# Keeping the two parts of split weights in DRAM across blocks, with the q-k-v staging and the weight sums moved

## The chip, the cores and the metric

The kernel runs on one core of a Trainium2 chip. The metric is the device time of one launch in microseconds (us), the median of three runs, lower being better.

## The reference

One step of a one-layer hybrid decoder, on a prompt of 2048 tokens and 32 sample tokens (8 sequences of 4), width 1024, in float32:

```python
h = rmsnorm(x, n1)
z = h @ w_in                      # splits into hq, hf, hi, hg, sq, sk, sv, ga, gb
f = lb + (1 - lb) * sigmoid(hf)
o_hg, s_new = hgrn_recurrence(hq, log(f), 1 - f, hi, s0, chunk=64)   # 4 heads of 128
y_a = (rmsnorm(o_hg, hg_norm_w) * silu(hg)) @ w_up_a
q, k, v = rotary(sq), rotary(sk), sv                 # 8 query heads, 2 key heads, of 64
y_b = sliding_window_attention_with_sinks(q, k, v, window=128) @ w_up_b
m = sigmoid(ga) * y_a + sigmoid(gb) * y_b
x = x + m @ w_o
x = x + square(relu(rmsnorm(x, n2) @ w_ff1)) @ w_ff2
y = rmsnorm(x, normf_w)
```

It also returns the last keys and values of the window and the recurrent states.

## The kernel before, in words

The prompt is cut into four blocks of 512 tokens, two to a superblock; block 3 carries the 32 sample tokens too. Every product is done in three matmuls of a rounded float32 format: a matrix is split into a high part (a cast) and a low part (what the cast leaves over), and high x high, low x high and high x low are added up. The activations are split as they are made; the weights are split each time that they are loaded.

A superblock runs as follows.

- The norm of its tokens, and their transposes. In superblock 0 the tiles of block 1 (`xo0` to `xo3`) follow block 0's: each is loaded, normed (a Square with sum on ScalarE, a scaling on ScalarE), transposed on TensorE, scaled into a buffer `ho` of which there is one, stored to DRAM as `hraw`, and added up with block 0's tile into the five operand sums of a Strassen product (`first_sums`: `zS1`, `zS2`, `zS3`, `zS4`, `zA22`). In superblock 1 these sums are made from `hraw`, loaded by POOL as `za11`, `za12`, `za21`, `za22`.
- The attention's k-v columns (`skv`, two weight units) and q columns (`sq`, four) of the even block, staged in a tile `zqk` and stored to DRAM.
- "z": the Strassen product of both blocks with the columns of `w_in` for the recurrence's queries and the two gates. Its weights are called `w1r` raw, `w1B` and `w1T` split; a phase that needs only the first activations and `w1B` comes first, then the one with the sums.
- The mixer of the even block: rotary and attention, `hi`, `hf`, `hg` (four units each), the recurrence, `ub` and `ua` (up-projections, four units each, with the gates: on VectorE the product with the gate at L1065, on POOL the addition of both at L1090), `wo` (eight units).
- The mixer of the odd block, which first makes `sq` and `skv` itself.
- The feed-forward part of both blocks, again by Strassen. The sums of its second weight matrix are made once, in block 0: sixteen sums, each of four loads (L508), four subtractions on VectorE (L510 to L513) and four stores to DRAM (L515), loads and stores issued by POOL.

A weight unit is 512 KB, a tile of 128x1024. It is loaded raw by SyncE (`r_...`, L144), cast by ScalarE to the high part (`h_...`, L230) and subtracted by VectorE to the low part (`l_...`, L231). All three tiles come from a pool of twelve. In the chip's program each engine works through its queue in order. A scheduler sets that order when the kernel is built, from the order of the code, the dependences and the free slots of the pools.

Of the kernel before, what the change touches and what calls it, by code (L numbers as in the profile page):

```python
# [38 lines left out]
def F(ap):  # L39
    return ap.bitcast(F32)  # L40
# [3 lines left out]
def tile_hybrid_step(  # L44
# [92 lines left out]
    v_last = cp.tile([P, P], F32, name="v_last")  # L137
    k_last = cp.tile([P, P], F32, name="k_last")

    def unit(parts, a, name):  # L140
        raw = wtile(F32, "r_" + name)
        raw3 = raw.rearrange("p (a b) -> p a b", a=a)
        for (p0, p1, src) in parts:
            nc.sync.dma_start(raw3[p0:p1], src)  # L144
        wh, wl = split_w(raw, name)
        return wh.rearrange("p (a b) -> p a b", a=a), wl.rearrange("p (a b) -> p a b", a=a)

    def split_w(raw, name):
        wh, wl = wtile(F32R, "h_" + name), wtile(F32R, "l_" + name)
        split_out(wh, wl, raw)  # L150
        return wh, wl
# [2 lines left out]
        nc.scalar.copy(hi, F(lo))  # L154
        nc.vector.tensor_tensor(lo, F(lo), F(hi), ALU.subtract)  # L155

    def unit_rows(w, k0, a, c0, nc_, name):
        src = w[k0 * P:(k0 + a) * P, c0:c0 + nc_].rearrange("(k p) c -> p k c", p=P)
        return unit([(0, P, src)], a, name)

    def gemm_T(ps, n, wts, acts, t0):
        nk = len(wts)
# [20 lines left out]
    def gemm_NK(w, c0, outs, acts, name, hook=None):  # L183
        for i in range(KD // 2):
            uh, ul = unit_rows(w, 2 * i, 2, c0, 512, f"{name}{i}")
            for (ps, r0, nr) in outs:
                for kk in range(2):
                    k = 2 * i + kk
                    lh = acts[k][0][:, r0:r0 + nr]
                    ll = acts[k][1][:, r0:r0 + nr]  # L190
                    nc.tensor.matmul(ps[0:nr], lh, uh[:, kk, :], start=(k == 0), stop=False)  # L191
                    nc.tensor.matmul(ps[0:nr], lh, ul[:, kk, :], start=False, stop=False)  # L192
# [332 lines left out]
    for bi in range(nblk):  # L525
# [70 lines left out]
        def colN512(c0, name, fn, hook=None):  # L596
            rings = [mm_ps, mm_ps, hg_ps, hg_ps, sw_ps]
            ps = [rings[i](f"ps_{name}_{t[3]}") for i, t in enumerate(tiles)]
            gemm_NK(w_in, c0, [(p, t[1], t[2]) for p, t in zip(ps, tiles)], h_acts, name, hook)
            for p, (kind, r0, nr, c) in zip(ps, tiles):  # L600
                fn(p[0:nr], kind, c, nr)

# [82 lines left out]
            return x.rearrange("p (g v d) -> p v g d", g=G, v=NKV)  # L685

        if not odd:
            stage = (op(3, F32, f"zqk_{B}") if sb else op(2, F32, f"zqk_{B}"))[:, 0:768 * ncb].rearrange("p (c e) -> p c e", e=768)

            def step():  # L690
                for _ in range(3):
# [1 line left out]
                        todo.pop(0)()  # L693

            def st_skv(ps, kind, c, nr):
                nc.scalar.copy(stage[:, c, 512:768], ps)

            def st_sq(ps, kind, c, nr):
                nc.scalar.activation(qk_out(stage[:, c, 0:512]), qk_in(ps), AF.Copy, scale=HD ** -0.5)
                nc.scalar.dma_start(zqk[sb][c * P:(c + 1) * P, :], stage[:, c, :])  # L700

            colN(C_SQ + 512, f"skv{B}", st_skv)
            colN512(C_SQ, f"sq{B}", st_sq, lambda i: step())
# [10 lines left out]
            with tc.tile_pool(name=f"zp{sb}", bufs=1, reuse_waits="tile") as zp:  # L714
                def z_fin(u, blk, x, ps=None):
                    o, nh = int(blk[1]) - 1, int(blk[2]) - 1
                    zi = 2 * u.n + nh
                    if zi >= HH:
                        nc.scalar.activation(x, x if ps is None else ps, AF.Tanh, scale=0.5)
                    elif ps is not None:  # L720
                        nc.scalar.copy(x, ps)
                    q = nc.scalar if zi >= HH else nc.gpsimd
                    rs = slice(zi * P, (zi + 1) * P)
                    c0, c1 = u.t0, u.t0 + u.ln
                    if o == 0:
# [342 lines left out]
        for j in range(KD):  # L1068
            if j % 2 == 0:
                ub = unit(  # L1070
                    [(kv * HD, (kv + 1) * HD, w_ub[kv * 256:(kv + 1) * 256, j * P:j * P + 256].rearrange("(k p) c -> p k c", p=HD)) for kv in range(NKV)],
                    4, f"ub{B}{j}")
# [9 lines left out]
        a_acts = [(oa[:, 0, k, :], oa[:, 1, k, :]) for k in range(4)]  # L1082
        mT = [op(2 + g, F32R, f"m{g}_{B}")[:, 0:8 * T].rearrange("p (s k t) -> p s k t", s=2, k=4) for g in range(2)]
        for j in range(KD):
            if j % 4 == 3:
                sum_next()
            if j % 2 == 0:
                ua = unit_rows(w_ua, 0, 4, j * P, 256, f"ua{B}{j}")
# [95 lines left out]
        if odd:  # L1184
            rings = (sw_ps, sw_ps, hg_ps, hg_ps, mm_ps)
            ps = [rings[i](f"wo{B}0_{t[3]}") for i, t in enumerate(tiles)]
            gemm_NK(w_o, 0, [(p, t[1], t[2]) for p, t in zip(ps, tiles)], m_acts, f"wo{B}0")
            for p, t in zip(ps, tiles):
                wo_out(t, p, 0)
            us_ = [unit_rows(w_o, 2 * i, 2, 512, 512, f"wo{B}1{i}") for i in range(KD // 2)]  # L1190
# [9 lines left out]
        else:  # L1200
# [21 lines left out]
            for cg in range(2):  # L1222
                rings = ((sw_ps, sw_ps, hg_ps, hg_ps), (mm_ps, mm_ps, sw_ps, sw_ps))[cg]
                ps = [rings[i](f"wo{B}{cg}_{t[3]}") for i, t in enumerate(tiles)]
                gemm_NK(w_o, cg * 512, [(p, t[1], t[2]) for p, t in zip(ps, tiles)], m_acts, f"wo{B}{cg}", hook)
                for p, t in zip(ps, tiles):
                    wo_out(t, p, cg)
            while todo:
# [293 lines left out]
```

## Time and profile before

| | us |
|---|---|
| Median of 3 runs | 2984.28 (2983.39 to 2984.38) |
| The profiled execution | 2989.63 |
| Its span, first to last instruction | 2987.9 |
| TensorE busy | 2825.5 (95%) |
| VectorE busy | 1775.6 (59%) |
| ScalarE busy | 1182.0 (40%) |
| POOL busy | 550.3 (18%) |

The mean granted clock of TensorE is 0.977 of its full speed. The DMA engines moved 492.78 MB. A time with no unit beside it is a position in the span, in us from its start: block 0's norms and q-k-v run to about 80, z of superblock 0 to 315, block 0's mixer to 560, block 1's to 830, the feed-forward part to 1495; z of superblock 1 to 1720, block 2's mixer to 2005, block 3's to 2285.

In the profile PE is TensorE, DVE VectorE, ACT ScalarE and SP SyncE; a q behind the name is the engine's sequencer, where DMAs are issued. In a timeline row stand the start, the duration, the engine, the line, the operation, output and inputs, and in brackets how long the engine had been idle and what released it. Names there are shortened: `h_ubb` is any of the block's `ub` units.

### The profile page before, as it was taken

The page shows a single profiled execution, that of the slowest core. Times are in us where ns is not written, and L with a number is a line of the kernel's source. Part 1 is how long each engine was busy: PE and PEld are TensorE (multiplying, and loading weights), DVE is VectorE, ACT ScalarE, POOL GpSimd, SP SyncE. Part 2 cuts the span into 40 slices and gives each one's busy share as a digit, 9 for nine tenths or more (in the row PEclk, how much of TensorE's full clock was granted, in tenths as well). Part 3 has the DMA queues.
Part 4 walks back from the last instruction along what each step waited for, and adds up shares of the span by engine and source line. Part 5 has one row for each costly group of instructions (what it writes and reads, how often), then busy time and mean ns, then how long its engine had stood idle before and what let it go on. Part 6 is the DMA issues. An engine that isn't in the chain of part 4 may idle for free. (4 is left out here: it accounts for less than half of the span.)

```text
span 2987.9 us, 50439 instructions
## 1 busy us (share of the span) xinstructions
PE 2825.5 (95%) x20087; PEld 2446.0 (82%) x20087; DVE 1775.6 (59%) x2877; ACT 1182.0 (40%) x2257; POOL 550.3 (18%) x957
## 2 busy tenths in 40 slices
PE   6799888999989999999999998999998999999998
PEld 5578666868878887888889967877887999999998
DVE  3664476457578775555575355525766877654446
ACT  3434332344343334554354443334424333344433
POOL 1130324121222221010220020120113333310001
PEclk8899899999999999999999999999998999999999
DMA  4473556424465447667563323442356444485552
GB/s 155 136 244 118 176 191 233 161 82 141 157 214 173 155 153 259 214 208 252 175 205 105 118 86 119 135 151 87 99 165 188 151 158 138 148 283 190 179 193 102
DMA packets 320180, 492.78 MB, mean 165 GB/s; under 512 B 28332, under 2 KB 193224, under 8 KB 319928
## 3 DMA queue, kind: packets, MB, share of 16 engines
q1 hardware_dynamic: 252048, 305.18, 32.5%
q0 software_dynamic: 48064, 155.58, 14.8%
q10 hardware_dynamic: 19832, 28.79, 2.7%
q8 instruction: 158, 2.59, 0.4%
q14 instruction: 78, 0.64, 0.1%
HBM read 351.96 MB, written 138.51 MB: 164 GB/s over the span
## 5 line engine op out<-in xcount | busy, mean ns | idle before, releaser
L1358 PE MATMUL f<-f2S,hw2T 128*128 128x264 f32 (+1 forms) x576 | 184.1, 320 | 0.0
L1360 PE MATMUL f<-f2S,lw2T 128*128 128x264 f32 (+1 forms) x576 | 183.5, 319 | 0.0
L1359 PE MATMUL f<-f2S,hw2T 128*128 128x264 f32 (+1 forms) x576 | 183.5, 319 | 0.0
L155 DVE TENSOR_TENSOR lw2T<-lw2T,hw2T 128x1024 fp32r<-128x1024 f32 x64 | 78.3, 1225 | 118.9 <-ACT hw2T L154 118.4
L238 PE MATMUL fB_f<-S,w1T_f 128*128 128x264 f32 (+1 forms) x384 | 123.1, 321 | 5.3 <-ACT c_f L300 4.4
L1358 PE MATMUL f<-f2A,h_w2B 128*128 128x264 f32 (+1 forms) x384 | 122.7, 320 | 0.5 <-ACT c_f L1251 0.5
L1359 PE MATMUL f<-f2A,h_w2B 128*128 128x264 f32 (+1 forms) x384 | 122.4, 319 | 0.1
L239 PE MATMUL fB_f<-S,w1T_f 128*128 128x264 f32 (+1 forms) x384 | 122.3, 319 | 0.0
L1360 PE MATMUL f<-f2A,l_w2B 128*128 128x264 f32 (+1 forms) x384 | 122.3, 319 | 0.0
L240 PE MATMUL fB_f<-S,w1T_f 128*128 128x264 f32 (+1 forms) x384 | 122.2, 319 | 0.0
L154 ACT CAST hw2T<-lw2T 128x1024 fp32r<-128x1024 f32 x64 | 67.2, 1050 | 132.8 <-DMA lw2T<-w_T 129.8
L1358 PEld LDWEIGHTS f<-f2S,hw2T 128*128 128x128 f32 x576 | 108.4, 188 | 7.6 <-DVE hw_ab L416 0.3
L1359 PEld LDWEIGHTS f<-f2S,hw2T 128*128 128x128 f32 x576 | 108.4, 188 | 7.3
L1360 PEld LDWEIGHTS f<-f2S,lw2T 128*128 128x128 f32 x576 | 108.0, 188 | 7.6
L155 DVE TENSOR_TENSOR f2S<-f2S 128x1024 fp32r<-128x1024 f32 (+1 forms) x64 | 79.3, 1241 | 54.7 <-ACT f2S L154 54.2
L231 DVE TENSOR_TENSOR l_w2B<-rw2B,h_w2B 128x1024 fp32r<-128x1024 f32 x48 | 58.8, 1225 | 81.6 <-ACT h_w2B L230 70.7
L230 ACT CAST w1T_f<-w1r_f 128x512 fp32r<-128x512 f32 x128 | 77.1, 619 | 70.5 <-PE fB_f L240 27.6
L231 DVE TENSOR_TENSOR w1T_f<-w1r_f,w1T_f 128x512 fp32r<-128x512 f32 x128 | 87.4, 688 | 23.9 <-ACT w1T_f L230 23.7
L1263 POOL DMA_DIRECT2D u_S<-s_f x144 | 77.7, 540 | 120.1 <-DVE s_f L1258 96.9
L1263 POOL DMA_DIRECT2D u_A<-c_f x104 | 56.2, 541 | 226.4 <-DVE c_f L1247 225.4
L154 ACT CAST f2S<-f2S 128x1024 fp32r<-128x1024 f32 (+1 forms) x64 | 68.0, 1064 | 53.0 <-DMA f2S<-u_S 52.9
L230 ACT CAST h_w2B<-rw2B 128x1024 fp32r<-128x1024 f32 x48 | 50.5, 1052 | 96.2 <-DMA rw2B<-w_ff 92.9
(833 smaller groups left out, 9684.3 us busy)
## 6 DMA issues: line engine op xcount, KB each, us to landing
w1r_f<-w_ff SPq DMA_DIRECT2D x64, 512.0 KB
lw2T<-w_T SPq DMA_DIRECT2D x64, 512.0 KB
rw2B<-w_ff SPq DMA_DIRECT2D x48, 512.0 KB
w1r_z<-w_in SPq DMA_DIRECT2D x40, 512.0 KB
f2S<-u_S SPq DMA_DIRECT2D x32, 528.0 KB
ws<-w_ff POOLq DMA_DIRECT2D x64, 256.0 KB, 4.8
r_wob<-w_o SPq DMA_DIRECT2D x32, 512.0 KB
f2S<-u_S SPq DMA_DIRECT2D x32, 512.0 KB
```

Of the source, the lines that this page charges most:

```text
L154: nc.scalar.copy(hi, F(lo))
L155: nc.vector.tensor_tensor(lo, F(lo), F(hi), ALU.subtract)
L230: nc.scalar.copy(dh, src)
L231: nc.vector.tensor_tensor(dl, src, F(dh), ALU.subtract)
L238: nc.tensor.matmul(ps, wh, ah, start=(first and k == 0), stop=False, skip_group_check=not first)
L239: nc.tensor.matmul(ps, wh, al, start=False, stop=False, skip_group_check=not first)
L240: nc.tensor.matmul(ps, wl, ah, start=False, stop=(last and k == 3), skip_group_check=not first)
L1263: nc.gpsimd.dma_start(us[o][u.n // 4][u.n % 4 * P:(u.n % 4 + 1) * P, u.t0:u.t0 + u.ln], y_)
L1358: nc.tensor.matmul(ps, wh, ah, start=first, stop=False, skip_group_check=cont)
L1359: nc.tensor.matmul(ps, wh, al, start=False, stop=False, skip_group_check=cont)
L1360: nc.tensor.matmul(ps, wl, ah, start=False, stop=lastk, skip_group_check=cont)
```

## The change

Three things are changed.

1. The units of `hi`, `hf`, `hg`, `ub`, `ua` and `wo` are split in block 0, those of `sq` and `skv` in block 1. Both parts are then stored to DRAM (`ws_...`, the high part on ScalarE's queue, the low part on POOL's), 34 units in all. The blocks after that load both parts, 2 x 512 KB, into the tiles `h_...` and `l_...`, with no raw tile, no cast and no subtraction. That holds for 96 units. The units of z and of the feed-forward part are loaded and split as before.
2. The staging of q, k and v of the even block was one tile in the slot of an activation operand (that of `zA22` in block 0, of `zS3` in block 2). It is now four tiles of the weight pool, one for each 128 tokens.
3. Ten of the sixteen sums are begun in z of superblock 0, where it was five, and block 0's mixer starts fewer by hand. The scheduler places the other six between z and block 0's gates.

```diff
+    wsd = {}
+
-    def unit(parts, a, name):
-        raw = wtile(F32, "r_" + name)
...
-        wh, wl = split_w(raw, name)
+    def unit(parts, a, name, key=None):
+        if key in wsd:
+            wh, wl = wtile(F32R, "h_" + name), wtile(F32R, "l_" + name)
+            nc.sync.dma_start(F(wh), wsd[key][0])
+            nc.sync.dma_start(F(wl), wsd[key][1])
+        else:
+            raw = wtile(F32, "r_" + name)
...
+            wh, wl = split_w(raw, name)
+            if key is not None:
+                wsd[key] = [tc.dram_tile([P, 1024], F32, name=f"ws_{key}_{i}") for i in range(2)]
+                nc.scalar.dma_start(wsd[key][0], F(wh))
+                nc.gpsimd.dma_start(wsd[key][1], F(wl))
...
-            wh, wl = unit_rows(w_in, 0, KD, c0 + h * P, P, name)
+            wh, wl = unit_rows(w_in, 0, KD, c0 + h * P, P, name, f"c{c0 + h * P}")
...
-            us = [unit_rows(w_in, 4 * i, 4, c0, 256, f"{name}{i}") for i in range(2)]
+            us = [unit_rows(w_in, 4 * i, 4, c0, 256, f"{name}{i}", f"c{c0}_{i}" if bi else None) for i in range(2)]
...
-            stage = (op(3, F32, f"zqk_{B}") if sb else op(2, F32, f"zqk_{B}"))[:, 0:768 * ncb].rearrange("p (c e) -> p c e", e=768)
+            stage = {}
...
             def st_skv(ps, kind, c, nr):
-                nc.scalar.copy(stage[:, c, 512:768], ps)
+                stage[c] = wtile(F32, f"zqk_{B}{c}")
+                nc.scalar.copy(stage[c][:, 512:768], ps)
...
                 def z_hook():
-                    if sb == 0 and len(sums) > NP - 5:
+                    if sb == 0 and len(sums) > NP - 11:
...
-            if j % 4 == 3:
+            if odd and j % 4 == 3:
                 sum_next()
...
-                    todo += [lambda g=g, k=k: reload(g, k), sum_next]
+                    todo.append(lambda g=g, k=k: reload(g, k))
```

The callers of `unit` for `ub`, `ua` and `wo` pass a key in the same way.

Three places show how the instructions stand now. First ScalarE's queue at the start of block 0, before: the last splits of the first sums (`zS2_0` to `zS4_0` from `xo0`), then the cast of the second `skv` unit, the evictions of `skv` into the staging tile, and the first `sq` unit.

```order
L230 CAST zS2_0_408<-fs0_412 128x4x128
L230 CAST zS3_0_409<-hw_ab010_385 128x4x128
L230 CAST zS4_0_411<-hw_ab000_110 128x4x128
L230 CAST h_skvb01_242<-r_skvb01_240 128x1024
L696 COPY zqk_b0_233<-ps_skvb0_0_246 128x256
L696 COPY zqk_b0_233<-ps_skvb0_1_272 128x256
L696 COPY zqk_b0_233<-ps_skvb0_2_298 128x256
L696 COPY zqk_b0_233<-ps_skvb0_3_324 128x256
L230 CAST h_sqb00_356<-r_sqb00_354 128x1024
```

The same place after; `xo1_460` and `xo2_528` are the next tiles of block 1.

```order
L241 CAST zS4_0_414<-hw_ab000_110 128x4x128
L216 ACTIVATE hw_ab011_461,ss_ab011_463<-xo1_460 128x1024
L229 ACTIVATE xo1_460<-xo1_460,rs_ab011_465 128x1024
L241 CAST zA22_0_413<-hw_ab011_461 128x4x128
L241 CAST zS1_0_410<-fs1_483 128x4x128
L241 CAST zS2_0_411<-fs1_483 128x4x128
L241 CAST zS3_0_412<-hw_ab011_461 128x4x128
L241 CAST zS4_0_414<-hw_ab001_134 128x4x128
L241 CAST h_skvb01_241<-r_skvb01_239 128x1024
L216 ACTIVATE hw_ab012_529,ss_ab012_531<-xo2_528 128x1024
L229 ACTIVATE xo2_528<-xo2_528,rs_ab012_533 128x1024
L708 COPY zqk_b00_270<-ps_skvb0_0_245 128x256
```

The norm and the sums of `xo1` have moved ahead of the cast `h_skvb01`; those of `xo2` and `xo3` now stand ahead of `h_sqb00` too.

Second, VectorE's queue at the start of z in superblock 1, before: the subtraction of the last `sq` unit, then the sums from the `za` tiles, with the split of z's first weights (`w1B11_z1_0`) in second place.

```order
L231 TENSOR_TENSOR l_sqb23_11821<-r_sqb23_11818,h_sqb23_11820 128x1024
L452 TENSOR_TENSOR zs1b20_11865<-za21b20_11863,za22b20_11864 128x528
L231 TENSOR_TENSOR w1B11_z1_0_11963<-w1r0_z1_0_11961,w1B11_z1_0_11963 128x512
L453 TENSOR_TENSOR zs2b20_11866<-zs1b20_11865,za11b20_11861 128x528
L454 TENSOR_TENSOR za21b20_11863<-za11b20_11861,za21b20_11863 128x528
L455 TENSOR_TENSOR za12b20_11862<-za12b20_11862,zs2b20_11866 128x528
```

After, the end of these sums: 34 of their 36 operations stand ahead of that split.

```order
L464 TENSOR_TENSOR zs2b23_12008<-zs1b23_12007,za11b23_12003 128x528
L465 TENSOR_TENSOR za21b23_12005<-za11b23_12003,za21b23_12005 128x528
L466 TENSOR_TENSOR za12b23_12004<-za12b23_12004,zs2b23_12008 128x528
L242 TENSOR_TENSOR zS1_1_11926<-zs1b23_12007,zS1_1_11926 128x528
L242 TENSOR_TENSOR zS2_1_11927<-zs2b23_12008,zS2_1_11927 128x528
L242 TENSOR_TENSOR w1B11_z1_0_12033<-w1r0_z1_0_12031,w1B11_z1_0_12033 128x512
L242 TENSOR_TENSOR w1B21_z1_0_12037<-w1r0_z1_0_12031,w1B21_z1_0_12037 128x512
```

The splits of `w1B` have moved from among the sums to behind nearly all of them.

Third, POOL's queue at the gates of block 0, before: the additions of the gates (`ga_b0`) with the stores of the last sum between them.

```order
L1090 TENSOR_TENSOR ga_b0_3550<-ga_b0_3550,pb_b0_2694 128x512 x2
L515 DMA w2_T3_227<-ws15t_6206 128x512
L1090 TENSOR_TENSOR ga_b0_3550<-ga_b0_3550,pb_b0_2694 128x512
L515 DMA w2_T1_225<-ws1501_6200 128x512
L1090 TENSOR_TENSOR ga_b0_3550<-ga_b0_3550,pb_b0_2694 128x512
L515 DMA w2_T2_226<-ws1511_6204 128x512
L515 DMA w2_T4_228<-ws1510_6202 128x512
L1090 TENSOR_TENSOR ga_b0_3550<-ga_b0_3550,pb_b0_2694 128x512
```

After, the stores of the low parts of `ua` and `wo` (`ws_ua...`, `ws_wo...`) stand there.

```order
L156 DMA ws_ua6_1_3997<-l_uab06_3993 128x1024
L156 DMA ws_wo00_1_4053<-l_wob000_4049 128x1024
L1102 TENSOR_TENSOR ga_b0_3686<-ga_b0_3686,pb_b0_2814 128x512 x4
L156 DMA ws_wo01_1_4090<-l_wob001_4086 128x1024
L1102 TENSOR_TENSOR ga_b0_3686<-ga_b0_3686,pb_b0_2814 128x512
L156 DMA ws_wo02_1_4127<-l_wob002_4123 128x1024
L1102 TENSOR_TENSOR ga_b0_3686<-ga_b0_3686,pb_b0_2814 128x512 x2
L156 DMA ws_wo03_1_4164<-l_wob003_4160 128x1024
```

The last sum's stores have moved ahead of the gates, and a `wo` unit's store stands between the additions in their stead.

More of the change, by code (lines that the diff above doesn't have):

```diff
@@ L155, in split_in, with unit_rows @@
         nc.vector.tensor_tensor(lo, F(lo), F(hi), ALU.subtract)
-    def unit_rows(w, k0, a, c0, nc_, name):
+    def unit_rows(w, k0, a, c0, nc_, name, key=None):
         src = w[k0 * P:(k0 + a) * P, c0:c0 + nc_].rearrange("(k p) c -> p k c", p=P)
-        return unit([(0, P, src)], a, name)
+        return unit([(0, P, src)], a, name, key)
     def gemm_T(ps, n, wts, acts, t0):
@@ L181, in gemm_N, with gemm_NK @@
             nc.tensor.matmul(ps[0:nr, 0:n], ll, wh, start=False, stop=(k == nk - 1))
-    def gemm_NK(w, c0, outs, acts, name, hook=None):
+    def gemm_NK(w, c0, outs, acts, name, hook=None, key=None):
         for i in range(KD // 2):
-            uh, ul = unit_rows(w, 2 * i, 2, c0, 512, f"{name}{i}")
+            uh, ul = unit_rows(w, 2 * i, 2, c0, 512, f"{name}{i}", key and f"{key}{i}")
             for (ps, r0, nr) in outs:
@@ L598, in colN512 @@
             ps = [rings[i](f"ps_{name}_{t[3]}") for i, t in enumerate(tiles)]
-            gemm_NK(w_in, c0, [(p, t[1], t[2]) for p, t in zip(ps, tiles)], h_acts, name, hook)
+            gemm_NK(w_in, c0, [(p, t[1], t[2]) for p, t in zip(ps, tiles)], h_acts, name, hook, f"c{c0}_" if bi or c0 == C_HI else None)
             for p, (kind, r0, nr, c) in zip(ps, tiles):
@@ L695, in st_skv @@
             def st_skv(ps, kind, c, nr):
-                nc.scalar.copy(stage[:, c, 512:768], ps)
+                stage[c] = wtile(F32, f"zqk_{B}{c}")
+                nc.scalar.copy(stage[c][:, 512:768], ps)
             def st_sq(ps, kind, c, nr):
-                nc.scalar.activation(qk_out(stage[:, c, 0:512]), qk_in(ps), AF.Copy, scale=HD ** -0.5)
-                nc.scalar.dma_start(zqk[sb][c * P:(c + 1) * P, :], stage[:, c, :])
+                nc.scalar.activation(qk_out(stage[c][:, 0:512]), qk_in(ps), AF.Copy, scale=HD ** -0.5)
+                nc.scalar.dma_start(zqk[sb][c * P:(c + 1) * P, :], stage[c][:, 0:768])
             colN(C_SQ + 512, f"skv{B}", st_skv)
@@ L1071, in tile_hybrid_step @@
                     [(kv * HD, (kv + 1) * HD, w_ub[kv * 256:(kv + 1) * 256, j * P:j * P + 256].rearrange("(k p) c -> p k c", p=HD)) for kv in range(NKV)],
-                    4, f"ub{B}{j}")
+                    4, f"ub{B}{j}", f"ub{j}")
             for _ in gate(j, ub, b_acts, lambda j, t0, n: pb[:, j, t0:t0 + n], "b"):
                 pass
-            if j % 4 == 3:
+            if odd and j % 4 == 3:
                 sum_next()
@@ L1084, in tile_hybrid_step @@
         for j in range(KD):
-            if j % 4 == 3:
+            if odd and j % 4 == 3:
                 sum_next()
             if j % 2 == 0:
-                ua = unit_rows(w_ua, 0, 4, j * P, 256, f"ua{B}{j}")
+                ua = unit_rows(w_ua, 0, 4, j * P, 256, f"ua{B}{j}", f"ua{j}")
             for t0, n, o in gate(j, ua, a_acts, lambda j, t0, n: ga[:, j, t0:t0 + n], "a"):
@@ L1186, in tile_hybrid_step @@
             ps = [rings[i](f"wo{B}0_{t[3]}") for i, t in enumerate(tiles)]
-            gemm_NK(w_o, 0, [(p, t[1], t[2]) for p, t in zip(ps, tiles)], m_acts, f"wo{B}0")
+            gemm_NK(w_o, 0, [(p, t[1], t[2]) for p, t in zip(ps, tiles)], m_acts, f"wo{B}0", None, "wo0")
             for p, t in zip(ps, tiles):
                 wo_out(t, p, 0)
-            us_ = [unit_rows(w_o, 2 * i, 2, 512, 512, f"wo{B}1{i}") for i in range(KD // 2)]
+            us_ = [unit_rows(w_o, 2 * i, 2, 512, 512, f"wo{B}1{i}", f"wo1{i}") for i in range(KD // 2)]
             wts = [(us_[k // 2][0][:, k % 2, :], us_[k // 2][1][:, k % 2, :]) for k in range(KD)]
@@ L1224, in tile_hybrid_step @@
                 ps = [rings[i](f"wo{B}{cg}_{t[3]}") for i, t in enumerate(tiles)]
-                gemm_NK(w_o, cg * 512, [(p, t[1], t[2]) for p, t in zip(ps, tiles)], m_acts, f"wo{B}{cg}", hook)
+                gemm_NK(w_o, cg * 512, [(p, t[1], t[2]) for p, t in zip(ps, tiles)], m_acts, f"wo{B}{cg}", hook, f"wo{cg}")
                 for p, t in zip(ps, tiles):
```

6 lines of the change are left out of this document (3 added, 3 removed).

## The prediction

> **What bounds the kernel now.** First the page's head, then the span cut into stages (columns: length, then the busy time of each engine with its instruction count, the granted TensorE clock, DMA share, GB/s).
>
> ```profile
> span 2987.9 us, 50439 instructions
> PE 2825.5 (95%) x20087; PEld 2446.0 (82%) x20087; DVE 1775.6 (59%) x2877; ACT 1182.0 (40%) x2257; POOL 550.3 (18%) x957
> ```
>
> ```profile
> 80.00:160.00 80.00, 61.11 (x240) 47.52 (x239) 48.49 (x77) 35.31 (x59) 14.39 (x21) 0.83 0.39 129
> 160.00:310.00 150.00, 140.15 (x598) 113.33 (x597) 80.62 (x122) 55.98 (x93) 24.42 (x44) 0.97 0.56 186
> 310.00:560.00 250.00, 218.38 (x1860) 168.81 (x1859) 155.19 (x257) 84.72 (x208) 81.52 (x134) 0.93 0.58 190
> 560.00:830.00 270.00, 266.92 (x2210) 213.14 (x2208) 158.37 (x264) 113.24 (x250) 51.33 (x75) 1.00 0.44 139
> 1720.00:2005.00 285.00, 272.44 (x2251) 215.77 (x2251) 145.28 (x243) 108.12 (x245) 55.02 (x89) 0.99 0.40 126
> 2005.00:2285.00 280.00, 272.10 (x2577) 225.62 (x2576) 172.32 (x352) 106.55 (x290) 42.53 (x61) 0.99 0.39 118
> ```
>
> TensorE is busy 95% of the span, and the change takes no matmul away. It can only win TensorE's idle time, and the half-clock time behind it, back, or add to them. Per stage the loss is idle time plus (1 - clock) times busy time: z0's first part (80 to 160) 18.9 + 10.4 = 29.3 us, z0's rest 9.9 + 4.2 = 14.1, block 0's mixer (310 to 560) 31.6 + 15.3 = 46.9, block 1's 3.1, block 2's (1720 to 2005) 12.6 + 2.7 = 15.3, block 3's 7.9 + 2.7 = 10.6. So the blocks in which the splits go have 29 us between them at most, and the places that the change re-orders, or loads with stores, have three times as much.
>
> What an idle time costs besides itself: the first row follows 10.96 us of idle TensorE, the others 2.19 and 3.25 us.
>
> ```profile
> 39.00:46.00 7.00, 5.85 (x26) 5.55 (x27) 1.81 (x3) 0.41 (x2) 0.00 (x0) 0.50 0.03 11
> 46.00:60.00 14.00, 12.07 (x74) 10.50 (x74) 5.33 (x5) 5.82 (x9) 0.00 (x0) 0.99 0.26 75
> 1806.00:1814.00 8.00, 7.58 (x178) 5.71 (x178) 7.53 (x15) 1.05 (x1) 0.00 (x0) 0.79 0.01 3
> 1855.00:1863.00 8.00, 7.59 (x50) 7.49 (x51) 3.10 (x9) 1.89 (x9) 1.20 (x2) 0.79 0.01 2
> ```
>
> Seven microseconds at 0.50 are 3.5 us lost after a long wait; 8 us at 0.79 are 1.7 us after a short one. The Trainium skill ("TensorE: Matmul & The Clock Gate", Part 1) has the clock fall only after an idle window of about 3.4 us. By that rule alone the short waits cost no clock, and block 2's term below would be -3 for -6; the two rows at 0.79 show a loss, and they decide.
>
> **The splits that go (blocks 1 to 3).** 96 units lose a cast on ScalarE and a subtraction on VectorE. Groups by line (count, then busy us and mean ns; idle before):
>
> ```profile
> L230 ACT CAST h_wob<-r_wob 128x1024 fp32r<-128x1024 f32 x32 | 33.5, 1048 | 32.6 <-DMA r_wob<-w_o 25.0 <-PE wob L192 4.4 <-DVE y_b L1177 1.9
> L231 DVE TENSOR_TENSOR l_ubb<-r_ubb,h_ubb 128x1024 fp32r<-128x1024 f32 x16 | 19.6, 1223 | 20.5 <-ACT h_ubb L230 20.5
> ```
>
> 96 x 1.05 = 101 us of ScalarE and 96 x 1.22 = 117 us of VectorE. Both lie beside TensorE, so nearly all of it is worth nothing. What is worth something is head-of-line blocking: a cast that waits for its load holds up what stands behind it in the same queue. Rows of the two worst cases, TensorE's restart first, then the chain of waits ahead of 1806.41:
>
> ```profile
> 409.86 1.04 ACT L230 CAST h_ubb<-r_ubb 128x1024 fp32r<-128x1024 f32 x1 [13.69 <-DMA r_ubb<-w_up_b]
> 413.14 0.63 PE L635 MATMUL lv_b0g<-W_b 128*32 128x16 f32 x32 [9.19 <-DVE W_b L572]
> 1806.41 0.45 PE L635 MATMUL lv_b2g<-W_b 128*32 128x16 f32 x32 [2.19 <-DVE W_b L572]
> 1855.41 1.83 PE L1011 MATMUL u_b2o<-SV_b,kn_b2o 128*128 128x128 f32 x7 [3.25 <-DVE on_b2o L976]
> ```
>
> ```profile
> 1796.61 6.43 DMA r_ubb<-w_up_b
> 1803.13 1.06 ACT h_ubb L230
> 1804.21 1.23 DVE l_ubb L231
> 1805.44 0.47 DVE W_b L571
> ```
>
> In block 2 the 2.19 us and their 1.7 of clock go whole; the 3.25 us at 1855 is the norm chain of `o_b2o`, of which I take a third with its clock (the chain begins behind an `r_uab` load too). I take 2.19 + 1.7 + 1.7 = -6, rounded up, between -1 (the forget gate's evictions are late next, released by TensorE itself) and -12. Block 3 has the same places with smaller losses: -4 of 10.6 (0 to -8). Block 1: -2 of 3.1 (0 to -3). Block 0's 9.19 stays, since block 0 still splits.
>
> **The doubled loads.** Each of the 96 units is read as 2 x 512 KB, 50 MB more. A stretch of z0 with TensorE never idle gives the matmul's pitch:
>
> ```profile
> 140.00:160.00 20.00, 20.00 (x89) 16.41 (x88) 9.41 (x15) 6.57 (x12) 2.70 (x5) 1.00 0.40 132
> ```
>
> 20.00 / 89 = 0.225 us, so the 24 matmuls of a unit (128x512) take 5.4 us, and 1.05 MB per 5.4 us is 194 GB/s where a unit drove 97. The stages from 560, 1720 and 2005 moved 139, 126 and 118 GB/s at shares of 0.44, 0.40 and 0.39, which puts a full share near 310. Adding 97 GB/s while units stream makes 0.7 to 0.75: hidden, at 0, with +8 as the upper end (the load of each first unit comes 1.5 us later, some six starts a block) and 0 as the lower, for the three tiles of a unit become two in the pool of 12, so loads start earlier.
>
> **Start of block 0: the staging tile moves the norms.** The staging gave up the slot of `zA22`, and the scheduler now puts the chains of `xo1` to `xo3` (norm, transpose, sums, splits; one `ho` buffer, so one after the other) ahead of the casts `h_skvb01` and `h_sqb00`, with TensorE's transposes likewise. Before, they ran during z0:
>
> ```profile
> 37.83 1.04 ACT L230 CAST h_skvb<-r_skvb 128x1024 fp32r<-128x1024 f32 x1
> 82.90 1.06 ACT L205 ACTIVATE hw_ab<-xo 128x1024 f32<-128x1024 f32 x1 [0.24 <-DVE zA L231]
> 95.34 0.62 ACT L230 CAST zS<-hw_ab 128x512 fp32r<-128x512 f32 x1 [4.08 <-DVE hw_ab L454]
> 97.75 1.06 ACT L205 ACTIVATE hw_ab<-xo 128x1024 f32<-128x1024 f32 x1 [0.23 <-DVE zS L231]
> 110.81 1.06 ACT L205 ACTIVATE hw_ab<-xo 128x1024 f32<-128x1024 f32 x1 [1.19 <-DVE zS L231]
> ```
>
> ```profile
> 38.92 0.79 PE L179 MATMUL ps_skvb<-h_skvb,hT 128*128 128x256 f32 x2 [10.96 <-ACT h_skvb L230]
> 53.31 0.73 PE L191 MATMUL ps_sqb<-h_sqb,hT 128*128 128x512 f32 x2 [1.41 <-ACT h_sqb L230]
> 115.09 1.33 PE L225 MATMUL tp_ab<-ident,xo 128*128 128x128 f32 x5 [7.90 <-ACT xo L218]
> ```
>
> A tile's chain takes 13.1 to 14.9 us from Square to Square. So `h_skvb01` is cast at about 37.8 + 13.7 = 51.5; the rest of k-v's matmuls (12 to 13 us) end at 65.6, with `xo2`'s second half waiting behind their evictions; then 9 us of `xo2` and 13 of `xo3`, and q's matmuls start near 89 where they started at 53.31: +36, and 3.5 us of clock. Against that, z0's first part no longer waits for these chains (7.90 at 115.09 is one): of its 29.3 us I leave 3. And 2 us of z0's later loss come back with an emptier ScalarE. 36 + 3.5 - 26.3 - 2 = +11. Lower end +2: three chains at 10 us each, without z0's casts between. Upper end +20: z0's first part loses 12 rather than 3, to the ten sums now begun in z0.
>
> **Block 0's mixer: sums out, stores in.** Five of the eleven sums in it go to z0 (20 subtractions and 40 POOL issues), and 28 units add an issue each on ScalarE and on POOL. Durations, and the wait in which the last sum lies:
>
> ```profile
> 512.58 0.69 DVE L510 TENSOR_TENSOR ws15t<-ws,ws 128x512 f32<-128x512 f32 x1
> 517.71 0.56 POOL L515 DMA_DIRECT2D w_T<-ws  x1 [1.46 <-DVE ws L511]
> 523.49 0.79 PE L191 MATMUL wob<-h_wob,m_b 128*128 128x512 f32 x1 [6.40 <-DVE ga_b L1065]
> 1510.59 0.33 ACTq L700 DMA_DIRECT2D zqk<-zqk_b  x1
> ```
>
> VectorE is relieved of 20 x 0.69 = 14 us, POOL of (40 - 28) x 0.56 = 7, ScalarE burdened with 28 x 0.33 = 9. The 6.40 us before 523.49 hold sum 15's four subtractions (2.8 us), which now come earlier; I credit -4 with the clock. Lower end -8: other waits of the stage, 25 us, shrink by a sixth. Upper end +12: a store of a low part waits on POOL for VectorE's subtraction, and behind it on POOL stand the loads of q-k-v and the gate's additions (L1090), which TensorE's 6.40 us hung on; 28 such stops at 0.4 us are 11. The stage's 190 GB/s at a share of 0.58 put a full share at 328; 29.4 MB of stores less 10.5 MB of sums over 250 us add 75 GB/s, share 0.81, short of full.
>
> **Start of z in block 2.** `zS3` no longer waits for the staging tile's stores, but the splits of z's first weights, in second place among VectorE's sums before, now stand behind 34 of their 36 operations.
>
> ```profile
> 1495.00:1530.00 35.00, 30.41 (x188) 26.74 (x187) 29.93 (x50) 19.99 (x38) 8.48 (x17) 1.00 0.80 269
> ```
>
> ```profile
> 1499.05 0.71 DVE L452 TENSOR_TENSOR zs1b<-za21b,za22b 128x528 f32<-128x528 f32 x1 [6.31 <-DMA za22b<-hraw]
> 1499.68 0.69 DVE L231 TENSOR_TENSOR w1B_z<-w1r_z,w1B_z 128x512 fp32r<-128x512 f32 x1
> ```
>
> ```profile
> 1510.34 0.39 PE L238 MATMUL fB_z<-hT,w1B_z 128*128 128x264 f32 x1 [1.09 <-ACT zqk_b L699]
> ```
>
> VectorE's 29.93 us over 50 are 0.60 each, 34 are 20.4 us. With the loads 3 us earlier than 1499.05 (four q splits of 1.22 less in VectorE's queue ahead), the first low part comes at 1496 + 20.4 + 0.6 = 1517; TensorE, ready at 1509, waits 8 and loses 3.5 of clock. The stage's 4.6 us of idle (35.00 - 30.41) go in exchange: +7. Ends: -4 (the sums run early, and all 4.6 are won) and +12 (no earlier load).
>
> **Sum.** 11 - 4 - 2 + 7 - 6 - 4 + 0 = +2, on the profiled execution's 2989.63 us: 2991.6. The median of the runs is 5.35 below the profiled one, so 2986.3. I forecast 2986.
>
> **Rivals.** *Faster.* The chains of `xo` at the start cost no more than they did later: at 10 us a tile, with all of z0's 29.3 us won, the start is -1 instead of +11; the splits' relief reaches its ends of -12 and -8 in blocks 2 and 3. With the other terms as they are that is +2 - 12 - 6 - 4 = -20: 2964. For it speaks that the chain before was stretched by z0's casts between its steps and a 4.08 us wait; against it, that the cast `h_skvb01` at 37.83 already came right behind one such chain with little beside it.
>
> *Slower, by one mechanism:* POOL's in-order stores in block 0. From a half microsecond of TensorE's waiting per store, 28 x 0.5 = +14 where I have -4: 3004. It decides the sign from 0 upwards, for +2 + 4 is the edge. For it: the gate's additions stand between eight `wo` stores, and POOL is the busiest there of all stages (81.52 us). Against: VectorE splits in order and soon. The Trainium skill ("DMA: Bandwidth & Descriptors", Rules for kernel authors) adds that queues of SP, ScalarE and GpSimd share the same 16 engines, so stores would take from the loads beside them; the shares above count all queues together, as it does, and 0.81 leaves room.
>
> *The splits stay hidden and the doubled loads are not:* each first unit late at the 8 us end, nothing won in blocks 1 to 3: +22, 3006. Against: shares of 0.4 to 0.45.
>
> **How the numbers follow.** Forecast 0.40, faster rival 0.28, stores 0.24, loads 0.08. A measurement here tells about 0.2% (6 us) from no change. The forecast's own range is 2972 to 3000: the half-widths of its terms (9, 10, 8, 5.5, 4, 4) added as squares give 17.5, of which I take four fifths. 0.24 of its 0.40 lie within 0.2%, 0.08 on either side. That gives faster 0.36, same 0.24, slower 0.40. The range to hold the time 8 times in 10 reaches to the two rivals: 2960 to 3006.
>
> **What would show it.** In the profile after: `h_skvb01` cast near 51 and q's matmuls from 85 to 92; the windows 80 to 160 with TensorE's clock near 1.00 from 95 on; a wait of 8 us ahead of z's first matmul in block 2, released by VectorE's `w1B`; ScalarE's waits for `r_ub` and `r_uab` gone after block 0. Wrong it would be if TensorE waits in blocks 1 to 3 on loads of `h_` and `l_` tiles, or if the waits of 310 to 560 grow beyond 47 us.

## The result, and the profile after

| | before | after |
|---|---|---|
| Median, 10 runs each (us) | 2982.24 (2977.53 to 2985.75) | 2996.91 (2990.56 to 3010.83) |
| Ratio to before, 95% interval | | 1.0055 (1.0038 to 1.0072) |
| Span of the profiled execution (us) | 2987.9 | 3009.0 |

The change costs half a per cent, some 15 us. The profiled execution is the slowest of the ten, as the one shown of before was above its median. So a second profile was taken of each: spans 3001.9 of the changed kernel (run `e4_after_again`) and 2981.2 of before (run `e5_before_again`).

The head of the page after:

```profile
span 3009.0 us, 50469 instructions
PE 2826.9 (94%) x20087; PEld 2449.7 (81%) x20087; DVE 1662.4 (55%) x2781; ACT 1089.9 (36%) x2161; POOL 558.7 (19%) x991
DMA packets 305716, 578.77 MB, mean 192 GB/s; under 512 B 30764, under 2 KB 156744, under 8 KB 305464
```

VectorE lost 113 us of work and ScalarE 92, close to the 117 and 101 that were counted, TensorE's work stayed, and the DMA engines moved 86 MB more. The stages after (columns as before; z0's two parts, its end, the four mixers, and z's start in superblock 1):

```profile
85.00:160.00 75.00, 74.79 (x319) 61.55 (x320) 34.59 (x52) 25.95 (x46) 4.35 (x9) 0.96 0.54 165
160.00:260.00 100.00, 95.65 (x412) 77.61 (x411) 66.32 (x106) 36.58 (x63) 32.37 (x60) 0.98 0.72 244
260.00:345.00 85.00, 63.63 (x254) 50.56 (x252) 28.67 (x39) 21.57 (x33) 18.46 (x35) 0.88 0.78 272
345.00:570.00 225.00, 204.32 (x1813) 159.20 (x1814) 139.68 (x235) 82.99 (x205) 73.42 (x116) 0.94 0.77 267
570.00:840.00 270.00, 263.69 (x2197) 210.88 (x2195) 126.43 (x236) 85.90 (x222) 51.79 (x81) 1.00 0.61 210
1505.00:1545.00 40.00, 28.85 (x151) 24.82 (x150) 28.13 (x47) 19.45 (x35) 7.13 (x14) 0.83 0.80 278
1740.00:2022.00 282.00, 270.71 (x2247) 214.32 (x2247) 105.44 (x209) 74.90 (x211) 51.23 (x88) 0.99 0.55 191
2022.00:2305.00 283.00, 276.34 (x2586) 227.72 (x2586) 145.27 (x330) 84.67 (x267) 39.91 (x61) 0.98 0.48 161
```

z0's first part runs all but unbroken (74.79 of 75, at a clock of 0.96), where idle time and clock cost 29 us before. Its end, 260 to 345, now loses 21 us of idle and 8 of clock. The mixers of blocks 1 to 3 move 43 to 71 GB/s more; TensorE idles 6.3, 11.3 and 6.7 us in them, where it idled 3.1, 12.6 and 7.9. Neither of the two signs of being wrong that the prediction named came: block 0's mixer, 345 to 570, loses 21 us of idle time and 12 of clock, less than 47, and the largest wait in blocks 1 to 3 (at 1868.91 below) is not for a load of `h_` or `l_`.

To see where time goes, the same TensorE instructions were matched in two traces, and the median difference of their starts was taken at the borders of the stages. What a stage adds (us), the changed kernel's second profile against each of the two of before:

| stage (position before) | foreseen | against the second of before | against the first |
|---|---|---|---|
| start and z0, to 240 | +11 | +2.6 | -0.4 |
| z0's end, 240 to 340 | in the term below | +23.4 | +14.0 |
| block 0's mixer, 340 to 540 | -4 | -10.3 | -10.9 |
| block 1's mixer, to 800 | -2 | +1.7 | +1.1 |
| feed-forward, to 1460 | 0 | +4.4 | +4.8 |
| z's start, 1460 to 1520 | +7 | +8.2 | +8.7 |
| z and block 2's mixer, to 1940 | -6 | -6.0 | -2.8 |
| block 3's mixer, to 2300 | -4 | -3.4 | 0.0 |

The two executions of the kernel before lie 10 us apart at z0's end and up to 14 later, and near that border the difference hangs on the place by some 4 us, so a stage is read from such a table only where both columns agree. They agree on four of some size: z0's end loses, block 0's mixer wins a part of it back, z's start loses, and the feed-forward part loses 4 to 5 us, which no term foresaw. Stores alone and loads alone, below, each lose some 4 there too against the second profile (800 to 1460); why stays open.

The start of the changed kernel and its large waits, TensorE's rows:

```profile
52.78 0.80 PE L190 MATMUL ps_skvb<-h_skvb,hT 128*128 128x256 f32 x2 [11.28 <-ACT h_skvb L241]
83.27 1.22 PE L202 MATMUL ps_sqb<-h_sqb,hT 128*128 128x512 f32 x2 [5.83 <-ACT h_sqb L241]
324.31 0.80 PE L249 MATMUL fB_z<-zA,w1T_z 128*128 128x512 f32 x1 [10.94 <-ACT c_z L311]
1529.80 0.59 PE L249 MATMUL fB_z<-hT,w1B_z 128*128 128x264 f32 x1 [8.75 <-ACT zqk_b L711]
1868.91 1.44 PE L1023 MATMUL u_b2o<-SV_b,kn_b2o 128*128 128x128 f32 x5 [5.52 <-ACT kn_b2o L1005]
```

The q matmuls start 30 us later than the 53.31 of before, and nothing of that is left by 160. The wait ahead of 324.31 comes from here (ScalarE, then two short windows):

```profile
321.87 1.04 ACT L241 CAST h_hfb<-r_hfb 128x1024 fp32r<-128x1024 f32 x1 [12.93 <-DMA r_hfb<-w_in]
```

```profile
310.00:315.00 5.00, 3.37 (x15) 2.44 (x13) 0.00 (x0) 0.00 (x0) 2.70 (x5) 1.00 1.03 394
315.00:320.00 5.00, 0.00 (x0) 0.00 (x0) 0.00 (x0) 0.00 (x0) 0.29 (x1) 0.57 1.03 416
```

The DMA engines are full, next to nothing computes for 5 us, and ScalarE stands at the cast of a weight unit with z0's evictions (`c_z`) behind it. In that stretch the queues carry the loads of `hi` and `hf`, the stores of `hi`'s two parts, two of the moved sums and the load of q-k-v.

### The profile page after: what moved, and what is told of

It reads as the page before. It is cut to its first block, busy times and chain, and to the rows that moved or that the text cites. A ratio compares the mean times of both kernels' runs of the same rounds, so it can differ in the third digit from the quotient of the medians.

```text
span 3009.0 us, 50469 instructions
## 1 busy us (share of the span) xinstructions
PE 2826.9 (94%) x20087; PEld 2449.7 (81%) x20087; DVE 1662.4 (55%) x2781; ACT 1089.9 (36%) x2161; POOL 558.7 (19%) x991
## 4 chain that ended last, share of the span: by engine, by line
PE 41%; DMA 3%; DVE 2%; issue 2%; POOL 2%; ACT 1%; POOLq 0%; SPq 0%; DVEq 0%; ACTq 0%
PE f L1371 3%; PE f L1370 3%; PE f L1372 3%; PE fB_f L249 2%; PE fB_f L251 2%; PE fB_f L250 2%; PE fB_z L249 1%; PE fB_z L251 1%; PE fB_z L250 1%; PE fD_f L251 1%; PE fD_f L249 1%; PE fD_f L250 1%; PE wob L202 1%; PE wob L203 1%; PE wob L204 1%
## 5 line engine op out<-in xcount | busy, mean ns | idle before, releaser
L241 ACT CAST w1B_f<-w1r_f 128x512 fp32r<-128x512 f32 x96 | 58.9, 621 | 81.9 <-DMA w1r_f<-w_ff 43.0
L249 PE MATMUL fB_z<-zS,w1T_z 128*128 128x264 f32 (+1 forms) x240 | 78.8, 328 | 9.8 <-ACT c_z L311 9.8
```

The lines of the kernel that those rows point to most:

```text
L241: nc.scalar.copy(dh, src)
L249: nc.tensor.matmul(ps, wh, ah, start=(first and k == 0), stop=False, skip_group_check=not first)
```

## The experiments

Each ratio is against the kernel before on the same chip, with its 95% interval; 0.1% is 3 us.

### Each part alone, and the changed kernel again

**Staging alone.** The change's edit of `stage`, `st_skv` and `st_sq`, on the kernel before:

```diff
-            stage = (op(3, F32, f"zqk_{B}") if sb else op(2, F32, f"zqk_{B}"))[:, 0:768 * ncb].rearrange("p (c e) -> p c e", e=768)
+            stage = {}
...
+                stage[c] = wtile(F32, f"zqk_{B}{c}")
```

> The kernel before with the q-k-v staging in weight tiles alone. My theory (each part has its own place): the start loses 33 us until q's matmuls and has them back by 140, and z of superblock 1 starts 8 to 9 us later, nothing else: +5 to +10 us. Rival (the loss comes from stored parts and sums, which crowd the DMA engines): 0 +- 3.

Measured 1.0025 (1.0013 to 1.0037), +7 us. The size is that of my theory, and the start's 31 us were indeed made up by 140. By matched starts the stage of z's start costs 4 to 5 us against either profile of before, for 8 to 9 expected, and in another place: z's first matmul follows at once, and the waits stand ahead of it, in q's matmuls from 1479 on (1.53, 1.85 and 1.23 us, for casts and subtractions of `sq` units). Where the rest lies its profile does not tell: its span, 2981.1, is that of the second profile of before.

**Stored parts alone.** The edit of `unit` with its keys, staging and sums as before.

> The kernel before with the parts stored and loaded alone (staging and sums as before). My theory: block 0 with its 28 MB of stores loses 0 to 8 us, blocks 1 to 3 win 3 to 5, together 0 to +5. Rival (stores on POOL and ScalarE hold the queues of block 0 up): +10 to +15. Second rival (the splits were worth something and only the other parts hide it): -6 to -10.

Measured 1.0085 (1.0070 to 1.0100), +25 us. All three expectations fell, mine too: stored parts cost more than the whole change does.

**Sums alone.**

```diff
-                    if sb == 0 and len(sums) > NP - 5:
+                    if sb == 0 and len(sums) > NP - 11:
...
-            if j % 4 == 3:
+            if odd and j % 4 == 3:
...
-                    todo += [lambda g=g, k=k: reload(g, k), sum_next]
+                    todo.append(lambda g=g, k=k: reload(g, k))
```

> The kernel before with the sums moved alone. My theory: the end of z0 (260 to 340) loses 5 to 15 us to five more sums' loads and stores beside the first weights of block 0, and block 0's mixer wins as much or a little more back: -6 to +4. Rival (the late sums sit on the gate's chain and cost more than in z0): -8 to -12.

Measured 1.0000 (0.9988 to 1.0012). In its profile the wait on the gates of block 0, which before's second profile has too,

```profile
510.60 0.80 PE L191 MATMUL wob<-h_wob,m_b 128*128 128x512 f32 x1 [6.40 <-DVE ga_b L1065]
```

is gone, and TensorE's start times there fall by some 11 us (from +3.4 to -7.5 against that profile). z0's end is some 12 us later against the second profile of before and some 4 against the first, so what it costs there is not settled; the sum is nothing, as my theory had it.

**The changed kernel again.**

> The changed kernel again, for a second profile and its spread. Theory: +14 us as measured, with z0's end 15 to 25 us late and z of superblock 1 some 9 us late in this profile as well. Rival (the profile shown was an outlier at 3011, and the delay at z0's end is its alone): z0's end within 5 us of before.

Measured 1.0069 (1.0053 to 1.0085). z0's end is 14 to 23 us later here as well, with a cast of `h_hfb` that waited 11.97 us for its load. It is no outlier.

### What of the stored parts costs

**The kernel before again.**

> The kernel before again, for a second profile to compare positions with: the first was taken in an execution 5 us above the median. Expected: span 2970 to 2985, with the waits of block 0 (413, 523) smaller by 5 to 10 us than in the first.

Span 2981.2. The wait at 523 was there again, 6.40 us; the one at 413 was 8.10. It was ahead at z0's end, by 10 us, so the second half of the expectation was wrong.

**Stores alone.** Units are stored, but none is loaded back:

```diff
-        if key in wsd:
+        if False:
...
-            if key is not None:
+            if key is not None and key not in wsd:
```

> Staging and sums as before; the 34 units are stored, but never loaded: all blocks split their raw weights as before. The output is the reference's. My theory now (the stores beside block 0's loads cost most of the 25 us of stored parts): +12 to +22 us. Rival (the doubled loads of blocks 1 to 3 cost it): 0 to +5.

Measured 1.0088 (1.0069 to 1.0107), +26 us: as much as stored parts with their loads, above my upper end.

**Loads alone.** One pair is stored and stands for all, so the kernel leaves the right weights out of blocks 1 to 3:

```diff
-                wsd[key] = [tc.dram_tile([P, 1024], F32, name=f"ws_{key}_{i}") for i in range(2)]
...
+                if 0 in wsd:
+                    wsd[key] = wsd[0]
+                else:
+                    wsd[0] = wsd[key] = [tc.dram_tile([P, 1024], F32, name=f"ws_{key}_{i}") for i in range(2)]
```

> Staging and sums as before; only the first unit's two parts are stored, and all 96 units of blocks 1 to 3 load that one pair, so every later product uses those weights and the output is not the reference's. Bytes, rows and issues of the loads are those of stored parts. My theory: the relief of splits and the doubled loads about cancel, -6 to +4. Rival (loads cost it): +10 to +20. Second rival (the splits' relief is worth what the prediction said, and only stores hide it): -10 to -15.

Measured 1.0036 (1.0023 to 1.0050), +11 us. 96 casts and 96 subtractions less, and still slower: the rival of the loads is nearer than my theory. All these loads read one place of 1 MB, where the changed kernel reads 34; what that does to them was not tested.

**Stores in block 1.** The changed kernel with the staging of before, and:

```diff
-            if key is not None:
+            if key is not None and bi > 0:
```

> The changed kernel with the staging of before, and the units split and stored in block 1 instead of block 0 (28 units, so 68 units load parts, and block 1 splits again). If stores cost by crowding block 0's DMA (share 0.8), block 1, whose share was 0.44 and where TensorE had 3 us of idle in all, takes them for nothing: -4 to +4 against before. Rival (a store costs wherever it stands, on the queues of POOL and ScalarE): +10 to +20.

Measured 1.0034 (1.0019 to 1.0049), +10 us. Against before's second profile block 0 ends 9 us earlier (the moved sums, without stores) and block 1 takes 16 us longer. So stores cost in a block that had a DMA share of 0.44, too, and my expectation of nothing fell.

### Bytes or issues

**Small stores.** The kernel of stores alone, with an eighth of each tile:

```diff
-                nc.scalar.dma_start(wsd[key][0], F(wh))
-                nc.gpsimd.dma_start(wsd[key][1], F(wl))
+                nc.scalar.dma_start(wsd[key][0][0:16, :], F(wh)[0:16, :])
+                nc.gpsimd.dma_start(wsd[key][1][0:16, :], F(wl)[0:16, :])
```

> The kernel of the run with stores alone, but each store moves 16 of 128 partitions (64 KB for 512 KB), never read. The order of TensorE, VectorE and SyncE is the same, and ScalarE and POOL issue the same stores with the same waits. Theory (the bytes crowd block 0's loads): most of the +26 us goes, +2 to +8 stays. Rival (the in-order issues and waits on POOL and ScalarE, or the order that they bring, cost it): +20 to +26 stays.

Measured 0.9981 (0.9964 to 0.9999) where full stores had 1.0088, below my theory's +2 to +8: the bytes cost some 32 us, and the issues on POOL and ScalarE with their waits for the splits, which are all still there, nothing. Block 0's mixer in the two profiles, small stores first:

```profile
310.00:560.00 250.00, 224.82 (x1895) 173.78 (x1894) 157.16 (x261) 92.14 (x218) 99.29 (x168) 0.94 0.66 215
```

```profile
310.00:560.00 250.00, 207.47 (x1802) 159.54 (x1802) 150.83 (x255) 82.60 (x205) 93.26 (x154) 0.92 0.80 282
```

67 GB/s and a share of 0.80 for 0.66 cost 17 us of TensorE in 250. The matched start times differ by 2 us at 280, 15 at 460 and 26 at 540. It comes to TensorE in some six steps. Two large ones are late loads at the head of a queue, of a weight unit on ScalarE and of a sum on VectorE. Each is shown as the wait for the load and the wait of TensorE behind it, full stores:

```profile
455.07 1.04 ACT L241 CAST h_uab<-r_uab 128x1024 fp32r<-128x1024 f32 x1 [6.54 <-DMA r_uab<-w_up_a]
457.15 1.22 PE L1022 MATMUL u_b0o<-SV_b,kn_b0o 128*128 128x128 f32 x4 [4.56 <-ACT kn_b0o L1004]
509.80 0.69 DVE L521 TENSOR_TENSOR ws13t<-ws,ws 128x512 f32<-128x512 f32 x1 [6.35 <-DMA ws<-w_ff]
512.35 0.80 PE L179 MATMUL yab<-oa_b,h_uab 128*128 128x512 f32 x1 [5.77 <-DVE ga_b L1076]
```

With small stores the two loads are waited for 2.84 and 3.80 us, and TensorE waits under 1 us in both places:

```profile
441.24 1.05 ACT L241 CAST h_uab<-r_uab 128x1024 fp32r<-128x1024 f32 x1 [2.84 <-DMA r_uab<-w_up_a]
488.26 0.69 DVE L521 TENSOR_TENSOR ws13t<-ws,ws 128x512 f32<-128x512 f32 x1 [3.80 <-DMA ws<-w_ff]
```

The last step, from 22 us to 26, full stores (TensorE, then ScalarE) and small ones (ScalarE):

```profile
556.86 0.80 PE L202 MATMUL wob<-h_wob,m_b 128*128 128x512 f32 x1 [8.10 <-DVE y_b L1188]
```

```profile
543.51 1.05 ACT L165 CAST hT_b<-hT_b 128x1024 fp32r<-128x1024 f32 x1 [7.95 <-DMA hT_b<-hraw]
```

```profile
517.53 1.05 ACT L165 CAST hT_b<-hT_b 128x1024 fp32r<-128x1024 f32 x1 [5.61 <-DMA hT_b<-hraw]
```

The cast of the next block's activations stands in ScalarE's queue ahead of the casts of `wo`, VectorE waits for those, and TensorE for VectorE's eviction, 8.10 us where it is 4.46 with small stores. Most of the 26 us between the two casts was there when the load was issued (535.13 and 511.50); the load itself took some 2 us longer.

A longer transfer also holds longer what waits for its landing, a tile for example: from 300 to 560 SyncE's waits that end with a landing add up to 36 us with full stores and 15 with small ones. This and the sharing of the DMA engines were not taken apart.

**A single load.** The kernel of loads alone, with one part for both, which leaves the low parts out as well:

```diff
-            wh, wl = wtile(F32R, "h_" + name), wtile(F32R, "l_" + name)
+            wh = wl = wtile(F32R, "h_" + name)
             nc.sync.dma_start(F(wh), wsd[key][0])
-            nc.sync.dma_start(F(wl), wsd[key][1])
```

> The kernel of the run with loads alone, but a unit of blocks 1 to 3 loads one part of 512 KB and uses it as both parts, so its output is not the reference's. No splits and no doubled bytes. Theory (the splits lay beside TensorE and were worth little; the doubled bytes ate what there was): -4 to 0, where loads alone has +11. Rival (the order that comes with the splits' absence costs it, not the bytes): +7 to +11. Second rival (the relief was worth the prediction's 12 us): -10 to -14.

Measured 0.9964 (0.9951 to 0.9977), -11 us, where two loads had 1.0036. The second rival held: without the splits and without doubled bytes the kernel gains what the prediction gave the splits, and the second 512 KB of each unit takes twice that away, 0.72% or 21 us. A unit also holds one tile of the pool here, where it holds two with loads alone and three in the kernel before, and it is one issue less, so its loads can run further ahead; these effects were not taken apart. Block 2's mixer in both, single loads first:

```profile
1720.00:2005.00 285.00, 280.39 (x2343) 220.15 (x2341) 112.08 (x231) 80.12 (x234) 48.11 (x81) 0.99 0.37 122
```

```profile
1720.00:2005.00 285.00, 272.53 (x2250) 215.65 (x2250) 105.88 (x209) 75.00 (x211) 51.28 (x88) 0.99 0.55 189
```

TensorE's idle time is 4.6 us and 12.5 us, at shares of 0.37 and 0.55. The largest wait of the doubled loads, on TensorE and on ScalarE, and the same cast with single loads:

```profile
1852.27 2.07 PE L1025 MATMUL u_b2o<-SV_b,kn_b2o 128*128 128x128 f32 x8 [5.07 <-ACT kn_b2o L1007]
```

```profile
1850.63 1.10 ACT L168 CAST hT_b<-hT_b 128x1088 fp32r<-128x1088 f32 x1 [6.65 <-DMA hT_b<-hraw]
```

```profile
1833.29 1.09 ACT L167 CAST hT_b<-hT_b 128x1088 fp32r<-128x1088 f32 x1
```

It is the wait of 1868.91 in the changed kernel. The weight casts that used to wait at the head of ScalarE's queue are gone, and the cast of the reloaded activations waits there instead: 11.6 us pass from the last issue of its load (1839.08) to the cast, and 4.4 with single loads (1828.90), where the cast does not wait. Between the two halves of that load SyncE issues both parts of a `ua` unit (1838.22 and 1838.65); with single loads `ua` was loaded earlier.

### The staging's two halves

**Staging in weight tiles in block 0 alone:**

```diff
+            if sb:
+                stg = op(3, F32, f"zqk_{B}")[:, 0:768 * ncb].rearrange("p (c e) -> p c e", e=768)
...
-                stage[c] = wtile(F32, f"zqk_{B}{c}")
+                stage[c] = stg[:, c, :] if sb else wtile(F32, f"zqk_{B}{c}")
```

> The changed kernel with the staging in weight tiles in block 0 alone; block 2 stages in the slot of before. Theory (the start's re-ordering costs nothing in the end, and z of superblock 1 loses 8 to 9 us): +10 to +12 against before, where the changed kernel has +19. Rival (the start costs it): +17 to +20.

**The staging of before in both:**

> The changed kernel with the staging of before in both superblocks. Theory: +10 to +12, the changed kernel's +19 less the +7 that staging alone cost. If the staging in block 0 has no part in it, this equals the run with staging split. Rival (with stores in block 0 the early sums of xo are what relieves the mixer, so that staging pays for itself there): +17 to +22.

Measured 1.0057 (1.0036 to 1.0077) and 1.0050 (1.0034 to 1.0066), +17 and +15 us, where both theories had +10 to +12. These intervals overlap each other and those of the changed kernel (1.0055 and 1.0069). What the staging costs beside the other parts, and whether block 0's half has a part in it, stays open. Only z's start can be read, with the staging of before in block 2 (split staging first):

```profile
1514.26 0.59 PE L249 MATMUL fB_z<-hT,w1B_z 128*128 128x264 f32 x1 [4.61 <-ACT zqk_b L713]
```

```profile
1513.20 0.39 PE L249 MATMUL fB_z<-hT,w1B_z 128*128 128x264 f32 x1 [3.18 <-ACT zqk_b L710]
```

Four to six microseconds of the changed kernel's 8.75 are the staging's, which agrees with the 4 to 5 of staging alone.

## Why the prediction was right or wrong

The forecast was 2986, with slower as the likeliest sign by a little (0.40, faster 0.36); 2996.91 is slower and lies in the range. For the mechanism that is luck: two costs that the sum held at or near nothing were worth 20 to 30 us each when taken singly, and the total missed by only some 13 us because the start came out better than foreseen and because the parts cost less together than apart.

**The doubled loads, taken at 0, were worth about +21.** This step failed. I compared the mean demand with the rate of a full share and called 0.7 to 0.75 hidden. The single load shows that a share of 0.55 already costs. What counted here was not whether the engines keep up on the mean, but how long one particular load took while others were in flight, when an in-order engine stood at its cast. The upper end of +8 had priced only the first weight unit of a stage; the largest wait of the doubled loads was for activations.

**The stores, inside block 0's -4, were worth +26 to +32.** I had both halves of this: the rival of the stores with +14, and the share of 0.81, to which the changed kernel's mixer came near with 0.77 and stores alone with 0.80. But I dismissed the share ("leaves room") and gave the rival the wrong mechanism. The in-order issues on POOL cost nothing, as small stores show; the bytes do. By the Trainium skill ("DMA: Bandwidth & Descriptors", Rules for kernel authors) the queues of SyncE, ScalarE and GpSimd run on the same engines. The runs agree: full stores, issued by ScalarE and POOL, made SyncE's load of `r_uab` late (a wait of 6.54 us for 2.84).

**The splits that go: -12 foreseen in blocks 1 to 3, -11 by the single load.** The size was right in all, and the mechanism (head-of-line casts) fits: TensorE's idle time in block 2 falls from 12.6 to 4.6 us, and the waits of 2.19 us at 1806 and 3.25 us at 1855 are gone. Where the gain lies was right only in part: by matched starts block 2 wins 11 to 12 us for 6 foreseen, block 1 some 2 for 2, block 3 1 to 5 for 4. A part of it may be due to the tiles that a unit no longer holds. In the changed kernel less of it appears, 3 to 9 us in blocks 2 and 3 by the table, since the longer loads put another cast in the same place.

**The start: +11 foreseen, about 0 measured.** The order was right and the times nearly: `h_skvb01` was cast at 51.69 for a foreseen 51.5, and q's matmuls began at 83.27, a little ahead of the foreseen 85 to 92. Both halves of the sum were off by some 5 us: q's start moved by 30 for 36, since `xo3`'s chain began at 72.16 for 74.6 and let q's cast through 10 us later, not 13, and 31 us came back by 140 for 26.

**z's start in superblock 1: +7 foreseen, +8 measured, by another release.** TensorE stood first behind the eviction of q's products, in the same place of ScalarE's queue behind a sum's cast that waits for a load:

```profile
1512.63 0.63 ACT L241 CAST zA<-za22b 128x528 fp32r<-128x528 f32 x1 [13.94 <-DMA za22b<-hraw]
1529.16 0.59 ACT L711 ACTIVATE zqk_b<-ps_sqb 128x512 f32<-128x512 f32 x1
```

VectorE's `w1B` was next, a 1.68 us wait at 1534.48, so the 34 operations ahead of z's weights would have held TensorE too. The loads were not 3 us earlier either, as I had taken them to be.

**The sums: their wait at the gates went, as foreseen,** and by the profiles z0's end gave 4 to 12 of the 11 us back. Parts alone do not add up: +7, +25 and 0 make +32, the change has +15 to +20, and stores and loads alone, +26 and +11, make +25 together. With stored parts the moved sums are worth more than alone: stored parts have 1.0085 without them and 1.0050 with them and the staging of before, intervals apart, which is 10 us, where the sums alone had no effect. The traces fit a mixer less crowded by the 10 MB that left it: against before's second profile stored parts without the sums add some 8 us at z0's end and 12 in block 0's mixer, the changed kernel 23 and then -10. That the bytes are the reason was not tested by itself.

Of the versions that leave nothing out, only the small stores came below the kernel before, by 0.2% at the edge of its interval, and their 64 KB serve no purpose; why they do so, with more instructions, is not known.

## What to carry to other kernels

Trading arithmetic on engines with slack for DMA traffic pays only if the traffic has more slack than they: 101 us of casts and 117 of subtractions lay beside TensorE and were worth 11 us, while the 50 MB of loads that replaced them cost 21 and 36 MB of stores some 30. A mean DMA share was no measure of room here; look which loads an in-order engine stands at, and price them at the landing time under the new traffic. Test such a change by shrinking the bytes of its transfers with all else kept, as the small stores did; the single load came near to that. These two runs told here what no reading of queues did.

## What the runs showed of the hardware

At a mean share of 0.80 in place of 0.66 (full and small stores) TensorE lost 17 us of 250, and at 0.55 in place of 0.37 (double and single loads) it lost 8 of 285, far below a full share. In the full stretch at 394 to 416 GB/s a 512 KB load that is issued at 305.40 reached its cast at 321.87, 16.5 us later. Full stores, issued by ScalarE and POOL, lengthened the waits for loads that SyncE issues (`r_uab`, 6.54 us for 2.84) and for loads that POOL issues (a sum's `ws`, 6.35 for 3.80).

What a short wait of TensorE costs in clock can be read more closely in the first trace of before. The granted clock falls to 0.50 for a stretch of 3.41 us or several, and these stretches lie on one grid. From 60 to 2300, each stretch at full clock in which TensorE idled more than 1.75 us was followed by one at 0.50, and none in which it idled less than 1.64. The stretch that ends at 1807.63 has the 2.19 us in it, and the clock is 0.50 from there to 1811.04. In the second trace of before two of 21 falls came after less, 0.54 and 1.41 us. So the waits of 2 to 3 us that the prediction priced with 1.7 us of clock each did cost it.
